# Weight tiles of 2048 columns in place of 1024 for the split into a rounded part and a remainder

## The chip, the cores and the metric

The kernel runs on one core of a Trainium2 chip, which stands alone on it. The metric is the device time of one execution in microseconds (us); the table below gives the median of three runs.

## What is computed

One layer of a hybrid decoder: 256 tokens of width 2048, in float32. A token mixer (an mLSTM group and an HGRN2 group that share one input projection and one output projection) and a SwiGLU network, each followed by a layer norm, each modulated by vectors that are worked out from a conditioning vector `c`. Cut to what matters here:

```python
mod = c_act @ w_mod[l] + b_mod[l]                       # 2048 x 12288
sh1, sc1, g1, sh2, sc2, g2 = jnp.split(mod[:, None, :], N_MOD, axis=-1)
u = x * (1.0 + sc1) + sh1
y = token_mixer(u, w_in[l], ..., w_out[l])              # u @ w_in, 2048 x 7176; y @ w_out, 2048 x 2048
x = layer_norm(DEEPNORM_ALPHA * x + (1.0 + g1) * y, ln1_g[l], ln1_b[l])
u = x * (1.0 + sc2) + sh2
y = swiglu(u, w_gate[l], w_up[l], w_down[l])            # 2048 x 5632 twice, 5632 x 2048
x = layer_norm(DEEPNORM_ALPHA * x + (1.0 + g2) * y, ln2_g[l], ln2_b[l])
```

## The kernel before

**Precision by splitting.** Weights and activations are float32. Each is written as a rounded part `h` and a remainder `l`, both in the type fp32r, and a product is the sum of three matmuls: rounded by rounded, rounded by remainder, remainder by rounded. So each weight passes through four steps: a DMA into a raw tile `wr` (on SyncE's queue, SP), a copy with rounding on ScalarE (ACT) into `wh`, the subtraction raw minus rounded on VectorE (DVE) into `wl`, and then the matmuls on TensorE (PE).

**Tiles.** Such a tile has 128 partitions and 1024 columns, 512 KB. There are 408 of them: 112 for the input projection, 32 for the output projection, 176 for gate and up, 88 for down. The pool of raw tiles has 4 buffers, those of `wh` and `wl` 5 each (line 56). A raw buffer comes free when the subtraction has read it; a `wh` or `wl` buffer when the last matmul on it is through. The helpers are `wtile` (line 203, input projection, two tiles for each 1 MB block of `in_win`) and `w1` (line 707, the other matrices); a copy shows in the profile as L128 with output `wh`, a subtraction as L213 (input projection) or L715 (the others), the loads as L208 and L710.

**Modulation.** 96 columns of `mod` are each made by loading a tile of 128x2048 of `w_mod` (1 MB, two buffers, `mr`) and one multiply-and-sum on VectorE over 2048 columns (L174). The first 32 feed `u` and have to be there before the input projection can use the rows they scale: `make_u` makes 128 rows of `u` (a scaled copy `t` and a rounding `uh` on ScalarE, a subtraction `ul` on VectorE). The other columns are spread over the later phases (`mods_some`, `some`).

**Phases.** The input projection starts with four rounds of 128 rows over the sections q and f (`fq_part`, eight PSUM banks; one round uses one 1 MB block, 48 matmuls of 256 columns), each round after the two modulation columns for its rows. Then come the sections qk, g, i and v for the same rows (`tile_part`: 1 MB blocks, again 48 matmuls of 256 columns, or 24 of 512 for i and v), then rows 512 to 1023, then the rest. PSUM is drained by ScalarE (or added up by VectorE) at the end of each block. The recurrences of HGRN2 and mLSTM run on VectorE, ScalarE and TensorE between the later blocks. Then the output projection (two passes over `c`, four column groups), the residual and the statistics of the first norm (`resid`, `stat`, `norm`), the transposes of the normed rows (`turn`, L817), gate and up for the first two groups together (`ffn_in((0, 1))`), the other nine groups (`up_to`), and down in two passes (`down`).

**Order.** Each engine works through its instructions in a fixed order, and so does SyncE, which issues all loads: an instruction that waits holds up all behind it. The order is set when the program is built, by a scheduler that takes the buffers of the pools and priorities into account; copies and subtractions of weights run under a raised priority (`PRI["w"]`).

Of the kernel before, what the change touches and what calls it, by code (L numbers as in the profile page):

```python
# [3 lines left out]
F32 = mybir.dt.float32  # L4
# [5 lines left out]
P = 128  # L10
# [42 lines left out]
PE_SECT = ()  # L53
DVE_SECT = ()
RATE = (0.45, 0.4, 0.5)
CFG = dict(big=10, med=10, wr=4, mr=2, wh=5, wl=5, s5=4, t=3, cm=2)


def win_plan():
# [20 lines left out]
def build(nc, tc, d):  # L80
    from contextlib import ExitStack

    with ExitStack() as ctx:
# [116 lines left out]
        def col(s, k):  # L200
            return modc[:, 16 * s + k : 16 * s + k + 1]

        def wtile(src, n=2048, cut=1024):
            for a in range(0, n, cut):
                m = min(cut, n - a)
                cnt[0] += 1
                r = wr.tile([P, 1024], F32, tag="w", name=f"wr{cnt[0]}")
                nc.sync.dma_start(r[:, :m], src[a // cut][:, :m])  # L208
                h = wh.tile([P, 1024], F32R, tag="h", name=f"wh{cnt[0]}")
                l = wl.tile([P, 1024], F32R, tag="l", name=f"wl{cnt[0]}")  # L210
                with tc.high_priority(PRI["w"]):
                    act(h[:, :m], r[:, :m], AF.Copy)
                    tt(l[:, :m], r[:, :m], h[:, :m].bitcast(F32), ALU.subtract)  # L213
                yield h, l

        def wraw(src):
            for a in range(2):
                cnt[0] += 1
                r = wr.tile([P, 1024], F32, tag="w", name=f"wr{cnt[0]}")
                nc.sync.dma_start(r, src[a])  # L220
                yield r, None

        def gN(bank, w, nk, n, u, k0, first, last):
            for b in range(n // P):
# [139 lines left out]
        def gates():  # L364
            raw = M(576, name="wg")
            nc.sync.dma_start(raw, d["wg"])
            h = wh.tile([P, 1024], F32R, tag="h", name="wgh")[:, :576]
            l = wl.tile([P, 1024], F32R, tag="l", name="wgl")[:, :576]
            with tc.high_priority(PRI["w"]):
                split(h, l, raw)  # L370
            o = psp.tile([P, 512], F32, tag="ps", name="gps")
# [332 lines left out]
                act(o[:, 512 * c : 512 * c + 512], bank, AF.Copy)  # L704
            return o

        def w1(src):
            cnt[0] += 1
            r = wr.tile([P, 1024], F32, tag="w", name=f"wr{cnt[0]}")
            nc.sync.dma_start(r, src)  # L710
            h = wh.tile([P, 1024], F32R, tag="h", name=f"wh{cnt[0]}")
            l = wl.tile([P, 1024], F32R, tag="l", name=f"wl{cnt[0]}")
            with tc.high_priority(PRI["w"]):
                act(h, r, AF.Copy)
                tt(l, r, h.bitcast(F32), ALU.subtract)  # L715
            return h, l

        def three(banks, h, l, a, b, first, last):
            for i, o in enumerate(banks):
                w = slice(512 * i, 512 * i + 512)  # L720
# [31 lines left out]
        def half(tiles, k, t):  # L752
            return tiles[k // 8][:, (k % 8) * T + t * P : (k % 8) * T + t * P + P]
# [4 lines left out]
        for part in (1, 0):  # L758
            for c in range(4):
                if part:  # L760
                    banks[c] = [ps(), ps()]
                tiles = []
                skew = part == 0 and c == 3
                for p in range(4):
                    tiles.append(w1(d["wo"][16 * (1 - part) + 4 * c + p]))
                    mods_some(RATE[2])
                    if not skew:
                        for t in range(2):
                            for j in range(2):
                                k = 8 * part + 2 * p + j  # L770
                                w = slice(512 * j, 512 * j + 512)
                                three([banks[c][t]], tiles[-1][0][:, w], tiles[-1][1][:, w], half(yh, k, t), half(yl, k, t), part == 1 and k == 8, part == 0 and k == 7)
                if skew:
                    for t in range(2):
                        for p in range(4):
                            for j in range(2):
                                k = 2 * p + j
                                w = slice(512 * j, 512 * j + 512)
                                three([banks[c][t]], tiles[p][0][:, w], tiles[p][1][:, w], half(yh, k, t), half(yl, k, t), False, k == 7)
                if part == 0:  # L780
                    for t in range(2):
                        resid(t, c, banks[c][t], G1, ALPHA)
                        stat(t, c)
# [105 lines left out]
        tc.add_manual_dep(table["load"], table["var"].name, order, reason="table")  # L889
        bk, held, block = ffn_in((0, 1))  # L890
        for k in range(2):
            for g in range(2):
                held[k, g] = w1(d["wf"][g * KT + k])
            block(k, 0)
        for c in range(4):
            turn(1, c)
# [2 lines left out]
        for k in range(2):  # L899
            block(k, 1)  # L900
        for k in range(2, KT):
            for g in range(2):
                held[k, g] = w1(d["wf"][g * KT + k])
            for t in range(2):
                block(k, t)
            some(2)
            for c in (2, 3):
                if k == 4 * c - 4:
                    some(max(0, len(late) - 8 * (3 - c)))
                    affine1(c)  # L910
                    make_u2(0, c)
                    make_u2(1, c)
# [15 lines left out]
        def up_to(gs):  # L928
            for g in gs:
                bk, held, block = ffn_in((g,))  # L930
                for k in range(KT):
                    held[k, g] = w1(d["wf"][g * KT + k])
                    for t in range(2):
                        block(k, t)
                    if k == 2:
# [10 lines left out]
        def down(k0, k1, G, last):  # L946
            for c in range(4):
# [7 lines left out]
                        three([bk[t]], held[k][0][:, w], held[k][1][:, w], hslice(k + j, t, 0), hslice(k + j, t, 1), k + j == k0, k + j == k1 - 1)  # L955

                for k in range(k0, k1, 2):
                    held[k] = w1(d["wd"][22 * c + k // 2])
                    if k < k1 - skew:
                        for t in range(2):  # L960
                            pair(k, t)
# [92 lines left out]
```

## Time and profile before

| what | us |
|---|---|
| median of 3 runs | 1266.17 (1265.77 to 1267.21) |
| the profiled execution, its own time | 1265.78 |
| its span, first to last instruction | 1264.0 |
| TensorE busy | 1212.8 (96%) |
| VectorE busy | 901.2 (71%) |
| ScalarE busy | 591.7 (47%) |
| DMA queue of the loads, share of the 16 engines | 74.9% |

The span is 1.8 us shorter than the time of the same execution. Matmuls are pipelined: the time of one matmul in the profile is longer than the distance to the next, so work on TensorE is counted below as matmuls times distance. TensorE is busy nearly always; VectorE is above 90% between 215 and 420 us and from 504 to 530 us, and at about half after 640 us. The granted clock of TensorE is 0.99 on the mean.

### The profile page before, as it was taken

To read this page: it belongs to the slowest core of one execution; us is meant where nothing else is said; L and a number is where in the kernel's file an instruction comes from. 1 tells how busy PE (TensorE), PEld (TensorE's weight loads), DVE (VectorE), ACT (ScalarE), POOL (GpSimd) and SP (SyncE) were. 2 spreads that over 40 slices of the span, in tenths; PEclk is the share of its full clock that TensorE was granted. 3 is DMA by queue.
4 is the path that set the end of the run, shared out by engine and by line. 5 is a ranking of instruction groups with operands and counts; after the bars stand their busy time and mean duration, and the time that the engine had idled before them with its cause. 6 is when DMAs were issued, how large, how long until landed. Compare 5 with 4: busy or idle time off the path is not lost.

```text
span 1264.0 us, 17132 instructions
## 1 busy us (share of the span) xinstructions
PE 1212.8 (96%) x6706; PEld 1040.0 (82%) x6706; DVE 901.2 (71%) x979; ACT 591.7 (47%) x743; POOL 3.9 (0%) x13
## 2 busy tenths in 40 slices
PE   4899999999999999799999999999999999999995
PEld 4888899997889887688888888888888888888884
DVE  6778997999999979997877554455555445445655
ACT  4554454835664644644544444433344444434340
POOL 0000000000000000000000000000000000000000
PEclk9999999999999999899999999999999999999998
DMA  9998997857788989889998666666666666676661
GB/s 364 386 335 328 341 398 285 301 200 264 267 327 308 330 317 334 305 320 327 324 329 325 192 190 189 178 194 191 198 191 192 189 194 185 193 256 184 191 191 66
DMA packets 75968, 328.00 MB, mean 260 GB/s; under 512 B 8432, under 2 KB 8816, under 8 KB 62704
## 3 DMA queue, kind: packets, MB, share of 16 engines
q1 hardware_dynamic: 75888, 326.92, 74.9%
q8 instruction: 52, 0.85, 0.3%
q14 instruction: 28, 0.23, 0.0%
HBM read 324.79 MB, written 2.10 MB: 259 GB/s over the span
## 4 chain that ended last, share of the span: by engine, by line
PE 89%; DVE 5%; ACT 3%; issue 2%; DMA 1%; DVEq 0%; ACTq 0%
PE ps L722 21%; PE ps L725 21%; PE ps L721 21%; PE ps L251 5%; PE ps L249 5%; PE ps L250 5%; PE ps L260 2%; PE ps L261 2%; PE ps L262 2%; DVE m L174 2%; PE ps L447 1%; ACT wh L128 1%; DMA m<-in_wmod 1%; DVE wl L213 1%; PE ps L863 1%
## 5 line engine op out<-in xcount | busy, mean ns | idle before, releaser
L128 ACT ACTIVATE wh<-wr 128x1024 fp32r<-128x1024 f32 x408 | 431.1, 1059 | 550.8 <-PE ps L722 426.2
L715 DVE TENSOR_TENSOR wl<-wr,wh 128x1024 fp32r<-128x1024 f32 x296 | 360.6, 1224 | 283.7 <-ACT wh L128 280.4
L721 PE MATMUL ps<-wh,u2h 128*128 128x512 f32 x704 | 275.6, 392 | 0.3 <-ACT s L128 0.3
L722 PE MATMUL ps<-wh,u2l 128*128 128x512 f32 x704 | 273.7, 389 | 0.1
L174 DVE CUSTOM_DVE_ANT_0 m<-m,cb,init 128x2048 f32<-128x2048 f32 x96 | 225.1, 2346 | 22.3 <-DMA m<-in_wmod 22.0
L725 PE MATMUL ps<-wl,u2h 128*128 128x512 f32 x704 | 217.0, 389 | 0.0
L249 PE MATMUL ps<-uh,wh 128*128 128x256 f32 x640 | 184.4, 292 | 22.5 <-ACT wh L128 17.1
L250 PE MATMUL ps<-ul,wh 128*128 128x256 f32 x640 | 181.8, 286 | 0.0
L251 PE MATMUL ps<-uh,wl 128*128 128x256 f32 x640 | 180.3, 287 | 1.1 <-DVE wl L213 1.0
L721 PEld LDWEIGHTS ps<-wh,u2h 128*128 128x128 f32 x704 | 132.6, 188 | 28.9 <-ACT s L128 0.7
L722 PEld LDWEIGHTS ps<-wh,u2l 128*128 128x128 f32 x704 | 132.0, 188 | 28.0 <-DVE u2l L838 0.8
L725 PEld LDWEIGHTS ps<-wl,u2h 128*128 128x128 f32 x704 | 132.1, 188 | 27.6
L213 DVE TENSOR_TENSOR wl<-wr,wh 128x1024 fp32r<-128x1024 f32 x112 | 135.8, 1221 | 25.1 <-ACT wh L128 24.5
L249 PEld LDWEIGHTS ps<-uh,wh 128*128 128x128 f32 x640 | 123.6, 194 | 25.0 <-ACT wh L128 17.8
L721 PE MATMUL ps<-wh,hid 128*128 128x512 f32 x352 | 137.2, 390 | 0.0
L725 PE MATMUL ps<-wl,hid 128*128 128x512 f32 x352 | 137.0, 389 | 0.0
L722 PE MATMUL ps<-wh,hid 128*128 128x512 f32 x352 | 137.0, 389 | 0.0
L250 PEld LDWEIGHTS ps<-ul,wh 128*128 128x128 f32 x640 | 124.5, 195 | 1.3 <-issue 1.0
L251 PEld LDWEIGHTS ps<-uh,wl 128*128 128x128 f32 x640 | 123.2, 194 | 1.9 <-DVE wl L213 1.8
L725 PEld LDWEIGHTS ps<-wl,hid 128*128 128x128 f32 x352 | 66.1, 188 | 13.9
L721 PEld LDWEIGHTS ps<-wh,hid 128*128 128x128 f32 x352 | 66.1, 188 | 13.6
L722 PEld LDWEIGHTS ps<-wh,hid 128*128 128x128 f32 x352 | 66.1, 188 | 13.6
(179 smaller groups left out, 1017.8 us busy)
## 6 DMA issues: line engine op xcount, KB each, us to landing
m<-in_wmod SPq DMA_DIRECT2D x96, 1024.0 KB, 7.1
wr<-in_wf SPq DMA_DIRECT2D x176, 512.0 KB, 4.2
wr<-in_win SPq DMA_DIRECT2D x112, 512.0 KB, 6.0
wr<-in_wd SPq DMA_DIRECT2D x88, 512.0 KB, 3.6
wr<-in_wo SPq DMA_DIRECT2D x32, 512.0 KB, 5.4
xT<-in_x SPq DMA_DIRECT2D x4, 512.0 KB, 8.0
z<-in_xr SPq DMA_DIRECT2D x2, 1024.0 KB, 8.6
out<-z SPq DMA_DIRECT2D x8, 256.0 KB, 2.4
```

The lines of the kernel that those rows point to most:

```text
L128: i = nc.scalar.activation(out, in_, f, **kw).ins
L174: table["mod"] = nc.vector.tensor_tensor_reduce(t, t, cb, 1.0, init[:, j : j + 1], ALU.mult, ALU.add, modc[:, j : j + 1]).ins
L213: tt(l[:, :m], r[:, :m], h[:, :m].bitcast(F32), ALU.subtract)
L249: mm(o, h[:, wsl], kt(uh, k0 + k), start=st, stop=False, skip_group_check=True)
L250: mm(o, h[:, wsl], kt(ul, k0 + k), start=False, stop=False, skip_group_check=True)
L251: mm(o, l[:, wsl], kt(uh, k0 + k), start=False, stop=en, skip_group_check=True)
L260: mm(o, a, h[:, w], start=first and k == 0, stop=False, skip_group_check=True)
L261: mm(o, a, l[:, w], start=False, stop=False, skip_group_check=True)
L715: tt(l, r, h.bitcast(F32), ALU.subtract)
L721: mm(o, a, h[:, w], start=first, stop=False, skip_group_check=True)
L722: mm(o, b, h[:, w], start=False, stop=False, skip_group_check=True)
L725: mm(o, a, l[:, w], start=False, stop=last, skip_group_check=True)
```

## The change

The helpers `wtile`, `wraw` and `w1` go; one helper `wide` takes one or two blocks of 1024 columns, loads each with a DMA of its own into one raw tile of 2048 columns, and rounds and subtracts the whole tile with one copy and one subtraction. It hands out halves of the two results. All loads keep their size and number (408 of 512 KB); copies and subtractions of weights go from 408 to 204 each. The pools change from 4, 5 and 5 buffers of 1024 columns to 2 (raw), 3 (rounded) and 2 (remainder) buffers of 2048. The input projection takes the two halves of a block of `in_win` as one tile, the first two groups of gate and up take the tiles of both groups for one k, the others those of two successive k, and the output projection and down two neighbouring tiles.

```diff
-CFG = dict(big=10, med=10, wr=4, mr=2, wh=5, wl=5, s5=4, t=3, cm=2)
+CFG = dict(big=10, med=10, wr=2, mr=2, wh=3, wl=2, s5=4, t=3, cm=2)
...
-        def wtile(src, n=2048, cut=1024):
...
+        def wide(*srcs):
+            cnt[0] += 1
+            n = 1024 * len(srcs)
+            r = wr.tile([P, 2048], F32, tag="w", name=f"wr{cnt[0]}")
+            for i, src in enumerate(srcs):
+                nc.sync.dma_start(r[:, 1024 * i : 1024 * i + 1024], src)
+            h = wh.tile([P, 2048], F32R, tag="h", name=f"wh{cnt[0]}")
+            l = wl.tile([P, 2048], F32R, tag="l", name=f"wl{cnt[0]}")
+            with tc.high_priority(PRI["w"]):
+                act(h[:, :n], r[:, :n], AF.Copy)
+                tt(l[:, :n], r[:, :n], h[:, :n].bitcast(F32), ALU.subtract)
+            return [(h[:, 1024 * i : 1024 * i + 1024], l[:, 1024 * i : 1024 * i + 1024]) for i in range(len(srcs))]
+
+        def wtile(src):
+            yield from wide(src[0], src[1])
...
-                    tiles.append(w1(d["wo"][16 * (1 - part) + 4 * c + p]))
+                    if p % 2 == 0:
+                        tiles += wide(*[d["wo"][16 * (1 - part) + 4 * c + p + i] for i in range(2)])
...
-            for g in range(2):
-                held[k, g] = w1(d["wf"][g * KT + k])
+            held[k, 0], held[k, 1] = wide(*[d["wf"][g * KT + k] for g in range(2)])
...
-                    held[k, g] = w1(d["wf"][g * KT + k])
+                    if k % 2 == 0:
+                        held[k, g], held[k + 1, g] = wide(*[d["wf"][g * KT + k + i] for i in range(2)])
...
-                    held[k] = w1(d["wd"][22 * c + k // 2])
+                    if (k - k0) % 4 == 0:
+                        held[k], held[k + 2] = wide(*[d["wd"][22 * c + k // 2 + i] for i in range(2)])
```

The scheduler lays the instructions out anew, and three places are of use below. In the names, `wl` is a remainder, `m` a tile of `w_mod` whose sum goes to `modc`, `t`, `uh` and `ul` the three steps of `make_u`.

VectorE, first two rounds of q and f, before:

```order
L213 TENSOR_TENSOR wl_143<-wr_140,wh_142 128x1024
L213 TENSOR_TENSOR wl_173<-wr_170,wh_172 128x1024
L174 ISA m_200,modc<-m_200,cb,init 128x2048
L174 ISA modc 128x1
L174 ISA m_203,modc<-m_203,cb,init 128x2048
L174 ISA modc 128x1
L213 TENSOR_TENSOR wl_213<-wr_210,wh_212 128x1024
L231 TENSOR_TENSOR ul_111<-t_206,uh_109 128x256
L213 TENSOR_TENSOR wl_243<-wr_240,wh_242 128x1024
```

VectorE at the same place, now:

```order
L213 TENSOR_TENSOR wl_144<-wr_140,wh_143 128x2048
L174 ISA m_195,modc<-m_195,cb,init 128x2048
L174 ISA modc 128x1
L174 ISA m_198,modc<-m_198,cb,init 128x2048
L174 ISA modc 128x1
L227 TENSOR_TENSOR ul_111<-t_201,uh_109 128x256
L213 TENSOR_TENSOR wl_209<-wr_205,wh_208 128x2048
L174 ISA m_260,modc<-m_260,cb,init 128x2048
```

A round's first half was subtracted ahead of `ul`; now the whole tile is subtracted behind it, and the next round's sums stand behind the whole tile.

ScalarE, where the sections q and f are drained and qk begins (`q`, `f`, `qk` from a PSUM bank `ps` are the drains), before:

```order
L128 ACTIVATE f_114<-ps_127 128x512
L128 ACTIVATE qk_117<-ps_431 128x512
L128 ACTIVATE wh_505<-wr_503 128x1024
L128 ACTIVATE qk_117<-ps_432 128x512
L128 ACTIVATE wh_535<-wr_533 128x1024
L128 ACTIVATE t_563<-xT_564,modc 128x256
L128 ACTIVATE uh_109<-t_563 128x256
L128 ACTIVATE wh_575<-wr_573 128x1024
L128 ACTIVATE qk_117<-ps_501 128x512
L128 ACTIVATE qk_117<-ps_502 128x512
L128 ACTIVATE wh_608<-wr_606 128x1024
```

ScalarE at the same place, now:

```order
L128 ACTIVATE f_114<-ps_127 128x512
L128 ACTIVATE qk_117<-ps_411 128x512
L128 ACTIVATE wh_481<-wr_478 128x2048
L128 ACTIVATE t_533<-xT_534,modc 128x256
L128 ACTIVATE qk_117<-ps_412 128x512
L128 ACTIVATE uh_109<-t_533 128x256
L128 ACTIVATE wh_546<-wr_543 128x2048
L128 ACTIVATE qk_117<-ps_476 128x512
L128 ACTIVATE qk_117<-ps_477 128x512
L128 ACTIVATE wh_608<-wr_605 128x2048
```

`wh_481` is the second tile of qk and `wh_546` the first of g: each copy of a whole tile now stands behind the drain of a block that TensorE works on.

VectorE at the end of the output projection (`s` and the first `z` are a residual, `st` the statistics, `mv` their sum, and the last two `wl` of each fence are weights of gate and up), before:

```order
L715 TENSOR_TENSOR wl_5016<-wr_5013,wh_5015 128x1024
L715 TENSOR_TENSOR wl_5034<-wr_5031,wh_5033 128x1024
L732 TENSOR_TENSOR s_4922<-ps_4512,bc_4246 128x512
L715 TENSOR_TENSOR wl_5040<-wr_5037,wh_5039 128x1024
L715 TENSOR_TENSOR wl_5118<-wr_5115,wh_5117 128x1024
L736 SCALAR_TENSOR_TENSOR z_4240<-z_4240,s_4922 128x512
L732 TENSOR_TENSOR s_4926<-ps_4513,bc_4246 128x512
L739 BN_STATS st_4244<-z_4240 128x6
L736 SCALAR_TENSOR_TENSOR z_4241<-z_4241,s_4926 128x512
L743 BN_AGGR mv_4944<-st_4244 128x2
L174 ISA m_5235,modc<-m_5235,cb,init 128x2048
```

VectorE at the same place, now:

```order
L174 ISA m_4853,modc<-m_4853,cb,init 128x2048
L174 ISA modc 128x1
L213 TENSOR_TENSOR wl_4651<-wr_4647,wh_4650 128x2048
L717 TENSOR_TENSOR s_4562<-ps_4202,bc_3966 128x512
L717 TENSOR_TENSOR s_4566<-ps_4203,bc_3966 128x512
L721 SCALAR_TENSOR_TENSOR z_3960<-z_3960,s_4562 128x512
L721 SCALAR_TENSOR_TENSOR z_3961<-z_3961,s_4566 128x512
L724 BN_STATS st_3964<-z_3960 128x6
L724 BN_STATS st_3965<-z_3961 128x6
L213 TENSOR_TENSOR wl_4670<-wr_4666,wh_4669 128x2048
L728 BN_AGGR mv_4584<-st_3964 128x2
L728 BN_AGGR mv_4630<-st_3965 128x2
```

Both halves of the tokens are now summed up together, and a second whole tile of weights stands between the statistics and their sum.

## Rows read from the trace of the kernel before

**Rows 1.** The page: engine, busy us (share of span) xinstructions

```profile
PE 1212.8 (96%) x6706; PEld 1040.0 (82%) x6706; DVE 901.2 (71%) x979; ACT 591.7 (47%) x743; POOL 3.9 (0%) x13
```

**Rows 2.** Waits of TensorE: who waited for whom, us, times, longest

```profile
PE ps L249 <- ACT wh L128: 17.1, 3, 16.7
PE ps L249 <- ACT uh L128: 5.3, 2, 3.8
PE ps L817 <- DVE z L810: 8.2, 1, 8.2
```

**Rows 3.** Busy time by stage: window, length, engines' busy us (xcount), clock, DMA share, GB/s

```profile
51.00:145.00 94.00, 91.26 (x577) 81.87 (x576) 79.94 (x81) 48.78 (x65) 0.74 (x1) 1.00 0.90 336
145.00:215.00 70.00, 70.00 (x586) 69.92 (x585) 58.78 (x58) 33.65 (x38) 0.74 (x1) 1.00 0.90 347
215.00:420.00 205.00, 200.85 (x1678) 180.23 (x1677) 194.61 (x256) 120.50 (x202) 0.00 (x0) 0.99 0.78 280
504.00:530.00 26.00, 17.42 (x77) 13.47 (x77) 25.97 (x40) 14.88 (x33) 0.00 (x0) 0.80 0.83 305
640.00:1245.00 605.00, 605.00 (x2714) 501.72 (x2713) 322.76 (x301) 250.97 (x257) 0.00 (x0) 1.00 0.65 201
```

**Rows 4.** Groups by line: engine, op, shapes, xcount, busy us, mean ns, idle before

```profile
L715 DVE TENSOR_TENSOR wl<-wr,wh 128x1024 fp32r<-128x1024 f32 x296 | 360.6, 1224 | 283.7 <-ACT wh L128 280.4 <-PE ps L863 3.0
L174 DVE CUSTOM_DVE_ANT_0 m<-m,cb,init 128x2048 f32<-128x2048 f32 x96 | 225.1, 2346 | 22.3 <-DMA m<-in_wmod 22.0
...
L128 ACT ACTIVATE wh<-wr 128x1024 fp32r<-128x1024 f32 x408 | 431.1, 1059 | 550.8 <-PE ps L722 426.2 <-DMA wr<-in_win 48.7 <-PE ps L250 38.4
```

**Rows 5.** Timeline, first 52 us, VectorE and ScalarE: start, length, instruction, idle before

```profile
15.57 1.99 ACT L128 ACTIVATE wh<-wr 128x1024 fp32r<-128x1024 f32 x2
...
18.92 2.34 DVE L174 CUSTOM_DVE_ANT_0 m<-m,cb,init 128x2048 f32<-128x2048 f32 x1
...
26.77 2.35 DVE L174 CUSTOM_DVE_ANT_0 m<-m,cb,init 128x2048 f32<-128x2048 f32 x1
29.27 2.35 DVE L174 CUSTOM_DVE_ANT_0 m<-m,cb,init 128x2048 f32<-128x2048 f32 x1
...
31.66 0.60 ACT L128 ACTIVATE t<-xT,modc 128x256 f32<-128x256 f32 x1 [0.18 <-DVE modc L174]
32.29 0.42 ACT L128 ACTIVATE uh<-t 128x256 fp32r<-128x256 f32 x1
...
35.80 2.35 DVE L174 CUSTOM_DVE_ANT_0 m<-m,cb,init 128x2048 f32<-128x2048 f32 x1 [0.88 <-DMA m<-in_wmod]
...
51.24 0.59 ACT L128 ACTIVATE f<-ps 128x512 f32<-128x512 f32 x1
```

**Rows 6.** Loads issued from 44 to 160 us: GB/s in 40 slices, us to landing

```profile
GB/s 429 407 424 384 205 424 362 136 429 370 353 348 268 340 326 381 374 387 158 394 401 384 407 316 376 360 143 410 233 403 364 384 266 251 370 291 347 398 333 400
...
wr<-in_win SPq DMA_DIRECT2D x40, 512.0 KB, 5.8
m<-in_wmod SPq DMA_DIRECT2D x17, 1024.0 KB, 7.0
```

**Rows 7.** Loads issued from 640 to 1240 us: xcount, KB each, us to landing

```profile
wr<-in_wd SPq DMA_DIRECT2D x88, 512.0 KB, 3.6
```

**Rows 8.** Timeline from 504 to 513 us: end of the output projection, first norm

```profile
504.05 2.35 DVE L715 TENSOR_TENSOR wl<-wr,wh 128x1024 fp32r<-128x1024 f32 x2
506.32 0.68 DVE L736 SCALAR_TENSOR_TENSOR z<-z,s 128x512 f32<-128x512 f32 x1
...
508.71 0.25 DVE L743 BATCH_NORM_AGGREGATE mv<-st 128x2 f32<-128x24 f32 x1
508.89 2.28 DVE L174 CUSTOM_DVE_ANT_0 m<-m,cb,init 128x2048 f32<-128x2048 f32 x1
...
511.70 1.89 DVE L810 TENSOR_SCALAR z<-z,mv 128x512 f32<-128x512 f32 x4
512.28 3.67 PE L817 MATMUL ps<-kc,z 128*128 128x128 f32 x16 [8.17 <-DVE z L810]
```

More of the change, by code (lines that the diff above doesn't have):

```diff
@@ L201, in col @@
             return modc[:, 16 * s + k : 16 * s + k + 1]
-        def wtile(src, n=2048, cut=1024):
[L204 to L221, printed above, removed]
+        def wide(*srcs):
[12 more added lines that the diff above has]
+            yield from wide(src[0], src[1])
         def gN(bank, w, nk, n, u, k0, first, last):
@@ L366, in gates @@
             nc.sync.dma_start(raw, d["wg"])
-            h = wh.tile([P, 1024], F32R, tag="h", name="wgh")[:, :576]
-            l = wl.tile([P, 1024], F32R, tag="l", name="wgl")[:, :576]
+            h = wh.tile([P, 2048], F32R, tag="h", name="wgh")[:, :576]
+            l = wl.tile([P, 2048], F32R, tag="l", name="wgl")[:, :576]
             with tc.high_priority(PRI["w"]):
@@ L705, in bcast @@
             return o
[L707 to L716, printed above, removed]
         def three(banks, h, l, a, b, first, last):
@@ L771, in build @@
                                 w = slice(512 * j, 512 * j + 512)
-                                three([banks[c][t]], tiles[-1][0][:, w], tiles[-1][1][:, w], half(yh, k, t), half(yl, k, t), part == 1 and k == 8, part == 0 and k == 7)
+                                three([banks[c][t]], tiles[p][0][:, w], tiles[p][1][:, w], half(yh, k, t), half(yl, k, t), part == 1 and k == 8, part == 0 and k == 7)
                 if skew:
@@ L901, in build @@
         for k in range(2, KT):
-            for g in range(2):
-                held[k, g] = w1(d["wf"][g * KT + k])
+            held[k, 0], held[k, 1] = wide(*[d["wf"][g * KT + k] for g in range(2)])
             for t in range(2):
@@ L931, in up_to @@
                 for k in range(KT):
-                    held[k, g] = w1(d["wf"][g * KT + k])
+                    if k % 2 == 0:
+                        held[k, g], held[k + 1, g] = wide(*[d["wf"][g * KT + k + i] for i in range(2)])
                     for t in range(2):
```

## The prediction

> **What bounds the kernel now.** I read the page's shares first, then what TensorE waits for, then the busy time by stage. TensorE is busy for 96% of the span [rows 1]. Its idle time is in few places [rows 2]: 16.7 us before the first matmul, some 5 us in the first rounds while u is made, and 8.2 us at the first norm; the rest is mostly the tail after the last matmul, where VectorE finishes the second norm. From 640 to 1245 us TensorE never idles, and VectorE works 323 of 605 us [rows 3]. Two stages are tight on both: from 51 to 145 us the loads take 0.90 of the DMA engines while TensorE idles only 2.7 us, and from 215 to 420 us VectorE is busy 194.6 of 205 us while TensorE idles 4.2 [rows 3]. So the reader should see that almost nothing is to be won on ScalarE or VectorE, and that TensorE stays fed because weights lie ready ahead: the copy into wh waits 426 us in all for TensorE to give a buffer back [rows 4], that is, the five buffers stand full.
>
> **What the change saves.** 204 copies and 204 subtractions fewer, at the same bytes and matmuls. A subtraction of 1024 columns takes 1.224 us, a VectorE operation on 2048 columns 2.346 [rows 4]; so a whole tile saves 2 x 1.224 - 2.35 = 0.1 us, 20 us of VectorE in the run. Two copies in a row take 1.99 us [rows 5]; I take 1.95 for a copy of 2048 and 2.3 for a subtraction. These savings lie beside TensorE's work wherever weights are ready ahead, so I cost them at nothing; where that cover is gone, they are inside the sums below.
>
> **What it costs.** A tile is usable only when its second load has landed and the whole copy is done, and remainders have 2 buffers: the next tile's subtraction cannot start before TensorE has left the tile before the present one. The lead falls from four tiles of 1024 (some 11 us) to one of 2048, minus its own subtraction (some 3 us).
>
> *First rounds (rows of u 0 to 511).* In the new order each round is a closed ring on VectorE and ScalarE: two sums, t, uh, ul, the whole copy (behind uh), the whole subtraction, and behind that the next sums. Sums: 4.6 us (2 x 2.28); t and uh 1.05; copy 1.95; subtraction 2.3; handovers 0.2: 10.1 us. Before, the sums of successive rounds begin at 18.92, 26.77 and 35.80, so 7.9 and 9.0 us apart, since half a tile was copied ahead of t and uh [rows 5]. The new first tile: copy from about 15.8 to 17.75, subtraction to 20.1; sums at 20.1, 30.2, 40.3; fourth copy from 40.3 + 4.6 + 0.1 + 1.05 = 46.05 to 48.0. TensorE runs 10 matmuls on the rounded part (1.2 us at 0.12 each, from 586 in 70 us [rows 3]), waits for the remainder until 50.35, then 38 more, 4.55 us: 54.9. Before, the last drain of this round starts at 51.24 [rows 5], right behind matmuls that end at about 50.5. **+4.4 us**; bounds 3 (a copy starts earlier than I have it) and 6 (sums' loads, 7.0 us to land [rows 6], come late).
>
> *51 to 145 us, the sections for the first rows.* Now two raw buffers make a ring: subtraction done, load issued, second half landed, copy, subtraction. A load of 512 KB lands after 5.8 us; at the best rate of the stage, 429 GB/s, the second half adds 1.2 [rows 6]. 0.1 + 5.8 + 1.2 + 1.95 + 0.1 + 2.3 = 11.45 us for two tiles, 5.7 each. TensorE needs 48 x 0.12 = 5.76 for a tile of q, f, qk or g, and 24 x 0.223 = 5.35 for one of i or v (0.223: 605 us over 2714 matmuls [rows 3]). The margin is nothing, and each drain (0.59 us [rows 5]) ahead of a copy or sum (2.35) ahead of a subtraction comes on top. I chained the sixteen tiles by hand in the new order with these durations: TensorE waits 1.4 us at the second tile of qk, 2.6 at the first tile of the second set of rows (its last u waits for two sums), and 0.2 to 1.6 at four more; 7.5 in all, where it loses 2.7 in idle time now and somewhat more in slow starts. **+4 us**, bounds 1 and 12 (half a microsecond a tile more).
>
> *145 to 215 us.* The same ring with one or two sums a round; TensorE does not idle here now [rows 3]. **+2**, bounds 0 and 5.
>
> *215 to 420 us.* In the new order VectorE has 62 us of work from the 38th subtraction to the 46th, while TensorE has 58 between the same tiles; over twenty tiles both are near 157. Without a lead of four tiles, bursts of the recurrences hit TensorE. The stage has no row for that; bounds are 0 and the 10.4 us in which VectorE idles today for its own dependencies [rows 3], if TensorE had to stand for as long. The stage's sums are nearly even, so I take the lower half: **+4**.
>
> *Output projection into the first norm.* In its last four column groups VectorE gets 2.3 + 2.35 + three steps of a residual (started 0.6 apart, as the row of z and the next in [rows 8]) = 6.45 us a tile against 5.4 on TensorE. With one tile of lead that puts the end of the projection back by 1.5. Then, today, TensorE stops at 504.1, the statistics are summed at 508.71, one more sum (2.28) comes first, and transposes start at 512.28, 8.17 us after the stop [rows 8]. In the new order the end of two sums of modulation (0.5), a subtraction (2.3), six residual steps (3.6), another subtraction (2.3), the sums of the statistics of both halves (0.5), one more sum of modulation (2.4) and the normalization (0.6) stand there: counted from the stop, the transposes start at 12.2. The second half of the tokens then follows 1.5 us closer, and one tile of gate and up comes 0.6 late. 1.5 + 4.0 - 1.5 + 0.6 = **+4.6**, bounds 0 (the sums find their place beside the matmuls) and 8.
>
> *640 us on.* Ring: 0.1 + 3.6 + 1.2 + 1.95 + 0.1 + 2.3 = 9.25 for two tiles [rows 7] against 2 x 24 x 0.223 = 10.7: **0**, covered by TensorE's own work; bounds 0 and +3 at the turns of groups. The tail after the last matmul is the same: **0**.
>
> Sum: 4.4 + 4 + 2 + 4 + 4.6 = 19 us on the profiled execution's 1265.8 (span 1264.0 and 1.8 around it), 0.4 under the median: **1285 us**.
>
> **A rule against and a rule for.** VectorE and ScalarE have idle time (71% and 47% busy [rows 1]), yet what TensorE waits for is their work. For such engines, not saturated but the cause of bubbles elsewhere, the Trainium skill, Perfetto Trace Analysis, section Optimizing Scalar/DVE Operations, advises to break instructions up; this change merges them, and by that rule the sum would be over zero, as mine.
>
> **Rivals.** *Faster: the saved fixed cost decides.* 0.1 us less for each tile on VectorE matters where it is full: 26 tiles from 215 to 420 us give 2.6, ten around the norm 1, and some of the 4.2 us of idle there could go; the first rounds could give 1 to 2. 1265.8 - 6 = 1260 us. Against it: TensorE idles little in those stages, and not for weights [rows 2, 3]. The Trainium skill, VectorE: DVE Perf Modes, section on the TRN2 errata, states that a single large tile pays the fixed latency once where many small ones pay it each; the two rows above agree on the sign. *No change: the first rounds' lag vanishes* because loads set the pace there and the later buffers, though fewer, suffice: 1266. Against it: the ring of the first rounds is longer than any load. *Slow everywhere: the two raw buffers bind in the long stage too.* If the second half lands 2 us later than in the sum above, the ring is 11.25 against 10.7, 0.27 us for each of 112 tiles from 640 us on, 30 us, and the earlier stages reach their upper bounds: 1265.8 + 30 + 25 = 1321. Against it: the loads use 0.65 of the DMA engines there.
>
> **How the numbers follow.** My forecast 0.80; faster 0.07; no change 0.08; slow everywhere 0.05. The measurement can tell about 0.2%, 2.5 us. The lower bounds of my terms give 4 us, the upper 34, but not all at one end: 1270 to 1302 holds the time 8 times in 10. Faster 0.07, within 0.2% 0.08, slower 0.85.
>
> **What would show it.** Right: sums of the first rounds about 10 us apart, drains of f ending near 55 us; waits of TensorE for copies or remainders of weights in many places from 51 to 215 us; VectorE's subtraction waiting for TensorE in place of ScalarE's copy; transposes of the first norm some 5 us later relative to their stage than the lag before; no idle TensorE after 640 us. Wrong: sums 8 to 9 us apart, TensorE without new waits before 215 us, or idle time in every tile of the down projection.

## The result, and the profile after

The changed kernel takes 1276.49 us (median of 4 runs, 1274.71 to 1277.16), the kernel before 1266.13 in the same comparison: a ratio of 1.0079 (95% interval 1.0067 to 1.0091), 10.4 us slower. The prediction was 1285 (1270 to 1302), slower with 0.85: the sign and the range held, the size was 8.5 us too high. The profiled execution of after has a span of 1275.3 us, 11.3 more than before.

The page of after, shares of the span and two groups by line (as [rows 1, 4]):

```profile
PE 1215.7 (95%) x6706; PEld 1042.5 (82%) x6706; DVE 879.5 (69%) x775; ACT 553.8 (43%) x539; POOL 3.9 (0%) x13
...
L213 DVE TENSOR_TENSOR wl<-wr,wh 128x2048 fp32r<-128x2048 f32 x204 | 467.2, 2291 | 305.5 <-PE ps L710 214.5
L128 ACT ACTIVATE wh<-wr 128x2048 fp32r<-128x2048 f32 x204 | 390.7, 1916 | 553.9 <-DMA wr<-in_wf 265.0
```

The change does what it says. VectorE works 21.7 us less and ScalarE 37.9 less than in [rows 1]; the subtraction now waits for TensorE (214.5 us) where the copy waited for it before [rows 4]. Neither engine's saving reaches the end. What TensorE waits for (as [rows 2]; us in total, times, longest), after:

```profile
PE ps L245 <- ACT wh L128: 25.0, 5, 17.4
PE ps L803 <- DVE z L796: 10.8, 1, 10.8
PE ps L247 <- DVE wl L213: 3.4, 3, 1.6
PE ps L706 <- DVE s L839: 2.7, 1, 2.7
PE ps L257 <- DVE wl L213: 2.3, 2, 1.2
```

The waits for copies rise from 17.1 to 25.0 us, but the 5.3 us for `uh` [rows 2] are gone: in the first rounds TensorE now waits for a copy that stands behind `uh`, so the two together grow by 2.6 us. Those for remainders (L247, L257) are 5.7 us against 2.3, and L706 is a wait that before did not have. The wait at the first norm (L803) is 10.8 against 8.17 us. By stage (as [rows 3], windows moved along with the lag):

```profile
55.00:149.00 94.00, 87.66 (x554) 79.18 (x554) 73.10 (x62) 45.54 (x47) 0.75 (x1) 0.98 0.83 317
149.00:220.00 71.00, 70.71 (x571) 69.71 (x570) 54.86 (x43) 27.98 (x23) 0.74 (x1) 1.00 0.92 351
220.00:425.00 205.00, 203.94 (x1719) 184.04 (x1718) 197.11 (x237) 123.04 (x183) 0.00 (x0) 1.00 0.78 283
650.00:1256.00 606.00, 606.00 (x2719) 502.61 (x2718) 309.32 (x192) 231.46 (x150) 0.00 (x0) 1.00 0.57 199
```

TensorE idles 6.3 of 94 us in the second stage (2.7 before), and its granted clock there is 0.98 of 2.4 GHz (1.00 before). It idles 1.1 us in the recurrences (4.2 before, so better), and never from 650 us on.

Where the time went is seen best by laying the traces side by side: both hold the same 5856 matmuls on weights, so the start of the n-th in one minus that in the other is the lag there. Its growth by stage, in us (stages by the time of the kernel before; e1 to e12 are the experiments; all from one profiled execution each, whose own time lies between 3.6 us under and 1.8 us over the median of its kernel, so small differences between sums say nothing):

| kernel | 0-50 | 50-143 | 143-302 | 302-321 | 321-484 | 484-591 | 591-638 | 638 on | sum |
|---|---|---|---|---|---|---|---|---|---|
| after | 4.1 | 4.9 | 0.1 | -5.0 | 0.8 | 1.9 | 4.6 | 0 | 11.4 |
| e1 halves | 0.7 | 2.5 | -0.1 | 1.6 | 0.7 | 0.4 | -0.1 | 0 | 5.7 |
| e2 whole in the input projection | 3.2 | 4.8 | 0.1 | -4.9 | 0.2 | -0.3 | -0.1 | 0 | 3.0 |
| e3 whole behind it | 0.6 | 2.4 | 0 | 0.5 | 1.0 | 2.1 | 0 | 0 | 6.6 |
| e4 1024, pools 4/6/4 | -1.4 | 0 | 5.9 | -5.0 | 0.9 | -1.0 | 0 | 0 | -0.6 |
| e5 product first | 4.5 | 3.4 | 0.2 | -5.0 | 0.6 | 1.4 | 1.5 | 0 | 6.6 |
| e6 third raw buffer | 3.9 | 4.8 | 0.5 | -1.2 | 0.6 | -2.4 | 0 | 0 | 6.2 |
| e7 third remainder buffer | 3.8 | 4.8 | 0.6 | -4.9 | 1.4 | 0.5 | 0 | 0 | 6.2 |
| e8 1024, products first | 2.4 | 0 | 0 | -3.7 | 1.0 | 0.8 | -0.1 | 0 | 0.4 |
| e9 order of the first rounds | 3.8 | 3.4 | 0.4 | -5.0 | 1.7 | 2.0 | 1.4 | 0 | 7.7 |
| e10 the same, on e2 | 6.2 | 3.5 | 0.2 | -4.9 | 0.6 | -1.1 | 0 | 0 | 4.5 |
| e11 halves, third raw buffer | -1.4 | 2.4 | 0.4 | 0.5 | 0.3 | -2.3 | 0 | 0 | -0.1 |
| e12 1024, asked for in pairs | 0.3 | 2.4 | 6.5 | -3.7 | 2.0 | 0.5 | 0 | 0 | 8.0 |

So after loses mainly in four places, gains in one, and the second half of the program is unchanged to 0.1 us.

### The profile page after: what moved, and what is told of

It is laid out like the page before. It is cut to its first block, busy times and chain, and to the rows that moved or that the text cites. A ratio compares the mean times of both kernels' runs of the same rounds, so it can differ in the third digit from the quotient of the medians.

```text
span 1275.3 us, 16453 instructions
## 1 busy us (share of the span) xinstructions
PE 1215.7 (95%) x6706; PEld 1042.5 (82%) x6706; DVE 879.5 (69%) x775; ACT 553.8 (43%) x539; POOL 3.9 (0%) x13
## 4 chain that ended last, share of the span: by engine, by line
PE 88%; DVE 7%; issue 2%; ACT 2%; DMA 1%; DVEq 0%; SPq 0%; ACTq 0%
PE ps L706 20%; PE ps L710 20%; PE ps L707 20%; PE ps L247 6%; PE ps L246 6%; PE ps L245 5%; DVE wl L213 3%; PE ps L257 2%; PE ps L256 2%; PE ps L258 2%; DVE m L174 2%; ACT wh L128 1%; PE ps L443 1%; DMA wr<-in_wo 1%; PE ps L849 1%
## 5 line engine op out<-in xcount | busy, mean ns | idle before, releaser
L213 DVE TENSOR_TENSOR wl<-wr,wh 128x2048 fp32r<-128x2048 f32 x204 | 467.2, 2291 | 305.5 <-PE ps L710 214.5
L128 ACT ACTIVATE wh<-wr 128x2048 fp32r<-128x2048 f32 x204 | 390.7, 1916 | 553.9 <-DMA wr<-in_wf 265.0
L706 PE MATMUL ps<-wh,u2h 128*128 128x512 f32 x704 | 275.9, 393 | 2.7 <-DVE s L839 2.7
L247 PE MATMUL ps<-uh,wl 128*128 128x256 f32 x640 | 177.8, 288 | 3.6 <-DVE wl L213 3.4
L706 PEld LDWEIGHTS ps<-wh,u2h 128*128 128x128 f32 x704 | 132.9, 189 | 30.8 <-DVE s L839 3.1
L706 PE MATMUL ps<-wh,hid 128*128 128x512 f32 x352 | 137.2, 390 | 0.0
L247 PEld LDWEIGHTS ps<-uh,wl 128*128 128x128 f32 x640 | 122.3, 196 | 5.1 <-DVE wl L213 4.5
L706 PEld LDWEIGHTS ps<-wh,hid 128*128 128x128 f32 x352 | 66.1, 188 | 13.6
L257 PE MATMUL ps<-wl,uh 128*128 128x512 f32 x128 | 50.2, 392 | 2.3 <-DVE wl L213 2.3
```

The source lines that it names most:

```text
L128: i = nc.scalar.activation(out, in_, f, **kw).ins
L213: tt(l[:, :n], r[:, :n], h[:, :n].bitcast(F32), ALU.subtract)
L247: mm(o, l[:, wsl], kt(uh, k0 + k), start=False, stop=en, skip_group_check=True)
L257: mm(o, a, l[:, w], start=False, stop=False, skip_group_check=True)
L706: mm(o, a, h[:, w], start=first, stop=False, skip_group_check=True)
```

## Experiments

Each ratio is to the kernel before, timed in the same comparison.

**e1, halves.** The pools of the change, but two copies and two subtractions for each tile:

```diff
-                act(h[:, :n], r[:, :n], AF.Copy)
-                tt(l[:, :n], r[:, :n], h[:, :n].bitcast(F32), ALU.subtract)
+                step = 1024
+                for a in range(0, n, step):
+                    s = slice(a, a + step)
+                    act(h[:, s], r[:, s], AF.Copy)
+                    tt(l[:, s], r[:, s], h[:, s].bitcast(F32), ALU.subtract)
```

> The changed kernel with its pools (2 raw, 3 rounded, 2 remainder buffers of 2048 columns), but each tile copied and subtracted in two halves of 1024 columns. Theory A (the length of the operations): it takes a whole copy of 1.9 us and a whole subtraction of 2.3 us to bring a tile to TensorE where two halves overlap, and what stands behind them on VectorE waits longer; with halves the lag of 4.1 us in the first rounds, the 4.9 us from 54 to 149 us, the 1.9 us at the first norm and the 4.6 us at the turn of the first groups go, and the time is 1261 (if the 4.9 us that the changed kernel gained near 310 us stay) to 1267. Theory B (the buffers): raw, rounded and remainder buffers come free only in pairs, so fewer loads run ahead; halves change nothing and the time is 1274 to 1278.

Measured 1.0024 (1.001 to 1.0037), 1269.65 us. TensorE's waits, e1:

```profile
PE ps L248 <- ACT wh L128: 16.6, 2, 16.3
PE ps L806 <- DVE z L799: 6.4, 1, 6.4
PE ps L248 <- ACT uh L128: 6.1, 2, 3.8
PE ps L493 <- DVE q L477: 3.6, 1, 3.6
```

Some 7 of the 10.4 us go, although the buffers are those of the change, so the pools alone do not make the loss (B falls). The wait at L706 is gone. In the first rounds TensorE waits 6.1 us for `uh`, where in after it waits 6.6 for copies. But the edit also lays out a new order, and the table shows that not all of the gain is the length of the operations (A): the 4.6 us at 614 us hang on order, as e3 and e5 show, and so do the 5.0 us near 310 us that are lost again here. Against A stand, too, the 2.5 us that stay from 50 to 143 us.

**e2 and e3, one part alone.** The loop of e1, with `nw` the count of tiles so far; e2, and e3 the other way round:

```diff
-                step = 1024
+                step = n if nw[0] <= 56 else 1024
```

> Whole tiles of 2048 columns in the input projection, as in the changed kernel; copies and subtractions in halves from the output projection on, same pools. Theory A: the first 150 us keep their 9 us, the gain of 4.9 us near 310 us stays, the losses at the norm (1.9) and at the turn of the first groups (4.6) go: 1266 + 9 - 4.9 = 1270, and 1269 to 1272 with what cannot be told. Theory B: 1274 to 1278, as the changed kernel.

> The other part alone: copies and subtractions in halves in the input projection, whole ones from the output projection on, same pools. Theory A: 1.9 us at the norm and 4.6 at the turn of the first groups on top of what the kernel with halves everywhere takes: that kernel plus 5 to 7 us. Theory C: those two losses were an accident of the order that the scheduler laid out, not of the tile's size; then it is within 2 us of the kernel with halves everywhere.

Measured 1.0021 (1.0012 to 1.0029) and 1.0045 (1.0033 to 1.0058). e2 came out as A had it: 3.2 + 4.8 - 4.9 and nothing behind. e3 is 2.7 us over e1 by the ratios, and the table shows why it is not the expected 5 to 7: whole operations take 2.1 us at the norm (0.4 with halves), but nothing at the turn of the first groups. There theory C is right: after's 4.6 us hang on its order.

**e4, 1024 columns with the bytes of the new pools.** `CFG`: wr=4, wh=6, wl=4.

> The kernel before with tiles of 1024 columns and pools of the bytes of the changed kernel: 4 raw, 6 rounded, 4 remainder buffers (5 and 5 before). Theory A: with short operations one remainder buffer less costs nothing: 1264 to 1268, and up to 5 us less if the stall of 3.1 us at 308.8 us goes with the order that is laid out anew. Theory B (the lead in remainders counts): 1270 or more, with waits of TensorE for remainders from 51 to 145 us.

Measured 1.0017 (1.0007 to 1.0028). One remainder buffer less loses nothing from 50 to 143 us (B falls), and near 310 us 5.0 us are gained with small tiles. What it loses instead is new: until 261.9 us TensorE waits 3.7 us for a product of the recurrence (L456) that the new order put behind a sum of modulation and a subtraction. Its profiled execution was the fastest of twelve, 3.6 us under the median, so the table shows it that much too well.

**e5, the product ahead.** In after, `swi`:

```diff
-            act(s, gate, AF.Silu)
-            tt(s, s, up, ALU.mult)
+            with tc.high_priority(PRI["w"] + 100):
+                act(s, gate, AF.Silu)
+                tt(s, s, up, ALU.mult)
```

> The changed kernel with one thing more: the SiLU copy and the product of gate and up (which free the PSUM banks) get a priority above the copies and subtractions of weights, so that at the turn from the first two groups to the third the first product stands ahead of the subtraction that it waited behind. Theory A: the loss of 4.6 us at 614 to 624 us (2.7 us of wait and the half clock behind it) hangs on one order of two instructions; it goes, and the time is 1276.5 - 4.6 = 1272 (ratio to the kernel before 1.0045). Theory B: VectorE is behind at this place as a whole, and TensorE then waits as long for the remainder that was moved back: 1275 to 1277.

Measured 1.0057 (1.0044 to 1.0069). The place in after, VectorE and TensorE:

```profile
612.14 2.35 DVE L174 CUSTOM_DVE_ANT_0 m<-m,cb,init 128x2048 f32<-128x2048 f32 x1 [4.09 <-DMA m<-in_wmod]
...
614.42 2.29 DVE L213 TENSOR_TENSOR wl<-wr,wh 128x2048 fp32r<-128x2048 f32 x1
...
616.63 0.68 DVE L839 TENSOR_TENSOR s<-s,ps 128x512 f32<-128x512 f32 x1
...
617.36 0.78 PE L706 MATMUL ps<-wh,u2h 128*128 128x512 f32 x1 [2.70 <-DVE s L839]
...
617.93 0.63 PE L707 MATMUL ps<-wh,u2l 128*128 128x512 f32 x1
```

The first two groups hold all eight PSUM banks; the third cannot start before a product has emptied one, and the product stood behind a sum (2.35) and a whole subtraction (2.29). Behind the wait of 2.70 us a matmul takes 0.63 in place of 0.39: the granted clock is 0.72 of 2.4 GHz from 616 to 622 us, thus the level of 1.2 GHz for a part of it. Busy time and clock of that stretch:

```profile
616.00:622.00 6.00, 4.64 (x13) 3.74 (x14) 5.68 (x7) 2.72 (x5) 0.00 (x0) 0.72 0.75 269
```

With the product ahead 1.5 of the 4.6 us stay, 1.3 of them a wait for the remainder that now comes later. Both theories are partly right. That e3, e6 and e7, with whole tiles here too, lose nothing in this place shows that tile size does not force it.

**e6 and e7, a third buffer.** After with med=8 and wr=3 (e6), or med=8 and wl=3 (e7).

> The changed kernel with a third raw buffer (8 instead of 10 small buffers of the med pool make room). Theory A1 (the ring of two raw buffers, load after subtraction, makes the 4.9 us from 54 to 149 us): a third buffer takes that away, the lag at 145 us falls from 9.0 to 4 or 5 us, and the time is 1272. Theory A2 (the order on ScalarE and VectorE makes it: a whole copy behind the scaled copies of u, a whole subtraction in one round with two sums): the lag at 145 us stays at 8 to 9 us, 1275 to 1277. The first rounds keep 4 us by both.

> The changed kernel with a third remainder buffer in place of a third raw one (8 med buffers again). Theory A1: as the subtraction no longer waits for TensorE, raw buffers come free earlier; 2 to 5 us less in the first 150 us, and the losses at the norm (1.9) and at the turn of the first groups (4.6) go, 1266 to 1271. Theory A2: the first 150 us keep 8 to 9 us; at the norm and the turn only the order decides, 1270 to 1277.

Measured 1.0058 (1.0045 to 1.0071) and 1.0041 (1.0028 to 1.0055). A1 falls in both: from 50 to 143 us both lose 4.8 as after does (4.9). They are faster than after only further on, where the order is laid out anew. TensorE's waits for remainders in e6 are those of after, to 0.2 us:

```profile
PE ps L247 <- DVE wl L213: 3.2, 3, 1.6
PE ps L257 <- DVE wl L213: 2.3, 2, 1.2
```

**e8, the stall of before taken away by order.** In the kernel before:

```diff
-                tt(k4[:, :, 0, :], k4[:, :, 0, :], d3[:, :, 1:2].broadcast_to([P, n, c]), ALU.mult)
-                tt(g4[:, :, 1, :], g4[:, :, 1, :], d3[:, :, 0:1].broadcast_to([P, n, c]), ALU.mult)
+                with tc.high_priority(PRI["w"] if c == 64 else 0): tt(k4[:, :, 0, :], k4[:, :, 0, :], d3[:, :, 1:2].broadcast_to([P, n, c]), ALU.mult)
+                with tc.high_priority(PRI["w"] if c == 64 else 0): tt(g4[:, :, 1, :], g4[:, :, 1, :], d3[:, :, 0:1].broadcast_to([P, n, c]), ALU.mult)
```

> The kernel before, tiles of 1024 columns, with one thing changed: in the recurrence of HGRN2 the two products of the last level get the priority of the weights, so that the second one no longer stands behind two subtractions where TensorE waits 3.1 us for it at 308.8 us. Theory A (the 4.9 us that the changed kernel gained there were an accident of order, not of the tile): most of it is gained here too, 1266 - 2.5 (wait) - up to 2.4 (half clock) = 1261 to 1264. Theory B (only fewer operations on VectorE can give it): the wait moves to the next place, 1265 to 1267.

Measured 0.9985 (0.9976 to 0.9994), 1265.0 us: the fastest of all, faster than both kernels. The time alone lies at the edge of B's range. The place is A's: the wait falls from 3.1 to 1.0 us, and 3.7 us are gained there. In the profiled execution 2.4 us are lost in the first rounds, with the instructions of before. What it takes away stands in the trace of the kernel before, VectorE and TensorE:

```profile
306.16 2.35 DVE L174 CUSTOM_DVE_ANT_0 m<-m,cb,init 128x2048 f32<-128x2048 f32 x1
...
308.43 1.22 DVE L213 TENSOR_TENSOR wl<-wr,wh 128x1024 fp32r<-128x1024 f32 x1
309.57 0.68 DVE L477 TENSOR_TENSOR kk<-kk,f 128x512 f32<-128x512 f32 x1
310.30 1.23 DVE L213 TENSOR_TENSOR wl<-wr,wh 128x1024 fp32r<-128x1024 f32 x1
311.44 0.68 DVE L478 TENSOR_TENSOR q<-q,f 128x512 f32<-128x512 f32 x1
...
312.27 1.46 PE L494 MATMUL ps<-q,kk 128*128 128x128 f32 x8 [3.10 <-DVE q L478]
```

The product q stood behind two subtractions. In after, only one sum of modulation stands ahead of the pair, and q comes with no subtraction in between. With tiles of 1024 columns e8, e4 and e12 gain 3.7 to 5.0 us here; with tiles of 2048 e1, e3, e6 and e11 have a wait of 3.5 or 3.6 us here again. The gain is one of order, not of the tile.

**e9 and e10, the order of the first rounds written out.** In after (e9) and e2 (e10), `fq_part` asks for the weights between the two sums of a round; `make_u` moreover ties its scaled copy behind the copy of the weights:

```diff
...
+                if 0 < k < 4:
+                    run(mod(16 + todo.pop(0)))
+                    first = table["mod"]
+                    win = list(next_win())
+                    tc.add_manual_dep(ahead["rem"], first.name, order, reason="weights")
+                    prep(k + 1)
+                    tc.add_manual_dep(table["mod"], ahead["rem"].name, order, reason="weights")
...
```

> The changed kernel, whole tiles everywhere, with the order of the first four rounds written out: the load and the copy of the next whole tile stand ahead of the scaled copy of u, and its subtraction between the two sums of a round. Theory A (the 4.1 us of the first rounds come from a ring in which a whole copy and a whole subtraction stand one behind the other after u): a round is then second sum 2.35, t and uh 1.05, copy beside the next first sum 2.35, subtraction 2.3, thus 8 us in place of 9.76, until the loads bind; the lag after the first rounds falls from 4.1 to between -1 and 1, and the time from 1276.5 to 1272 to 1274. Theory B (the longer wait for the second half of the load makes it): the lag stays at 3 to 4 us, 1275 to 1277.

> The kernel with whole tiles in the input projection alone and halves behind it, with the same order of the first four rounds. It was at 1.0021 of the kernel before without that order. Theory A: 3 to 4 us less, 1263 to 1266, at or under the kernel before. Theory B: 1268 to 1269, as without it.

Measured 1.0049 (1.0035 to 1.0063) and 1.0016 (1.0007 to 1.0025): the first rounds keep 3.8 and 6.2 us, not the -1 to 1 of A. The ring of operations was opened, and another wait took its place. SyncE's queue and ScalarE, e9:

```profile
14.53 7.81 SPq L173 DMA_DIRECT2D m<-in_wmod  x2
22.52 0.80 SPq L210 DMA_DIRECT2D wr<-in_win  x2
...
29.54 1.91 ACT L128 ACTIVATE wh<-wr 128x2048 fp32r<-128x2048 f32 x1 [1.65 <-DMA wr<-in_win]
```

The second of two loads of `w_mod` waits on SyncE's queue until its buffer is free at 22 us, and the loads of the next weights wait behind it, though their buffer is free from 19.7 us on, when its subtraction ended; the copy then waits for them, at 29.5 and again later. In that order the loads set the pace. That B (the second half alone) is right does not follow: the two orders differ in more than that.

**e11, halves with a third raw buffer.** e1 with med=8, wr=3.

> Halves everywhere with a third raw buffer (8 small buffers in place of 10). With halves and two raw buffers the copies wait for loads from 75 to 102 us, and 2.5 us are lost there. Theory A1 (with short operations the raw buffers that come free in pairs bind): those 2.5 us go, the lag at 145 us falls from 3.2 to about 1 us, and the time from 1269 to 1266 to 1267. Theory A2 (the loads' rate binds, whatever the buffers): 1268 to 1270.

Measured 1.001 (1.0001 to 1.0019). The time is near A1's, and yet A1 falls: 2.4 us are lost from 50 to 143 us as with two raw buffers; what it gains stands in the first rounds and at the norm.

**e12, tiles of 1024, asked for in pairs.** The kernel before with `return list(wtile(d["win"][i]))` in place of the generator.

> The kernel before, tiles of 1024 columns and its own pools (4, 5, 5), with one thing of the change: in the input projection the two tiles of a block are asked for together, so that both loads are placed in one go on the queue of loads and the loads of modulation columns stand behind both. Halves with the pools of the change lost 2.4 to 2.5 us from 54 to 149 us, with two raw buffers and with three. Theory P (buffers that come free in pairs make that loss): nothing is lost here in that stretch, the lag grows by under 1 us from the end of the first rounds to 145 us. Theory G (asking for two at once, and with it the order of the loads, makes it): the lag grows by 2 to 3 us there. What the recurrences do with the new order near 310 us is open; the time is between 1262 and 1270.

Measured 1.0047 (1.0035 to 1.006). From 50 to 143 us it loses the 2.4 us of e1 and e11, with small tiles and the pools of before: asking for two at once makes that loss (G). Through the order of the loads, as G has it, it does not come, as the trace shows. ScalarE, before:

```profile
74.64 1.06 ACT L128 ACTIVATE wh<-wr 128x1024 fp32r<-128x1024 f32 x1
78.25 0.60 ACT L128 ACTIVATE i<-ps 128x512 f32<-128x512 f32 x1 [2.56 <-PE ps L262]
```

and ScalarE and TensorE, e12:

```profile
78.01 0.60 ACT L128 ACTIVATE i<-ps 128x512 f32<-128x512 f32 x1 [3.07 <-PE ps L262]
78.50 1.05 ACT L128 ACTIVATE wh<-wr 128x1024 fp32r<-128x1024 f32 x1
...
79.61 0.73 PE L260 MATMUL ps<-wh,uh 128*128 128x512 f32 x2 [0.28 <-ACT wh L128]
80.87 0.50 PE L261 MATMUL ps<-wl,uh 128*128 128x512 f32 x1 [0.52 <-DVE wl L213]
```

Asking for both tiles of a block at once also puts their copies and subtractions in another place. Before, one more tile was copied ahead of the drain of i. In e12 a copy stands behind that drain, for which ScalarE waits 3.07 us for TensorE, and TensorE then waits for the copy and for its remainder. The same follows one block later, from 84.83 us on. The copies begin right behind the drains, so no load holds them up there. The order of the loads changes too (two loads of modulation columns stand together at 82.65 us), but no wait shows that it costs anything. Most of the rest of e12's loss has nothing to do with the tile: 6.5 us between 143 and 302 us, where L456 is late as in e4.

## Why the prediction was right, and where not

**First rounds, +4.4: measured 4.1.** The ring is there as worked out. VectorE and ScalarE of after (as [rows 5]):

```profile
19.63 2.35 DVE L174 CUSTOM_DVE_ANT_0 m<-m,cb,init 128x2048 f32<-128x2048 f32 x1
...
24.92 0.42 ACT L128 ACTIVATE uh<-t 128x256 fp32r<-128x256 f32 x1
25.25 1.90 ACT L128 ACTIVATE wh<-wr 128x2048 fp32r<-128x2048 f32 x1
...
27.18 2.29 DVE L213 TENSOR_TENSOR wl<-wr,wh 128x2048 fp32r<-128x2048 f32 x1 [1.38 <-ACT wh L128]
...
29.39 2.34 DVE L174 CUSTOM_DVE_ANT_0 m<-m,cb,init 128x2048 f32<-128x2048 f32 x1
...
39.14 2.35 DVE L174 CUSTOM_DVE_ANT_0 m<-m,cb,init 128x2048 f32<-128x2048 f32 x1
...
52.51 2.74 ACT L128 ACTIVATE f<-ps 128x512 f32<-128x512 f32 x4
```

Sums at 19.63, 29.39 and 39.14 against 20.1, 30.2 and 40.3 forecast; the last drain ends at 55.25, forecast 55. The ring was in fact shorter than forecast and TensorE slower: the remainder of the fourth tile is there at 49.03 us, forecast 50.35, and the 38 matmuls behind it take 5.4 us in place of 4.55, at a granted clock of 0.72 of 2.4 GHz from 46 to 52 us. In five profiles with whole tiles there and the scheduler's own order the term is 3.2 to 4.5; with small operations it is -1.4 to 2.4 in six. That spread is not one of order: e8 has the instructions of before in this stretch and is 2.4 us later, with a longer wait for u (4.8 against 3.8 us) and a granted clock of 0.72 against 0.86 from 40 to 52 us, so a difference of some 2 us in one profile of this stretch says nothing.

**51 to 145 us, +4: measured 4.9.** The largest waits came where I had chained them by hand. ScalarE and TensorE of after:

```profile
57.54 0.60 ACT L128 ACTIVATE qk<-ps 128x512 f32<-128x512 f32 x1 [2.28 <-PE ps L247]
58.03 1.90 ACT L128 ACTIVATE wh<-wr 128x2048 fp32r<-128x2048 f32 x1
...
62.31 0.39 PE L247 MATMUL ps<-uh,wl 128*128 128x256 f32 x1 [1.46 <-DVE wl L213]
...
102.11 0.39 PE L245 MATMUL ps<-uh,wh 128*128 128x256 f32 x1 [0.95 <-ACT wh L128]
...
104.44 0.39 PE L247 MATMUL ps<-uh,wl 128*128 128x256 f32 x1 [1.58 <-DVE wl L213]
```

At the second tile of qk the whole copy stands behind a drain that waits for TensorE, and TensorE waits 1.46 us (forecast 1.4). At the first tile of the second set of rows the whole copy stands behind `t` and `uh`, which wait for two sums, and TensorE waits 0.95 and 1.58 us (forecast 2.6). In all it idles 6.3 us in the stage, against 7.5. What was wrong is the ring: I let two raw buffers bind, and a third moves none of these waits (1.46, 0.95 and 1.59 us in e6). The 2.4 us of e1, e11 and e12 are another loss and no part of the 4.9: they arise from 79 to 88 us, where after has no wait.

The match of 4 and 4.9 is in part luck, since some 1.4 us of it are TensorE's clock, for which no term of the sum stands. e5 has the instructions of after in the same order up to 320 us and the same waits at this place, and loses 3.4. Busy time and clock, after and then e5:

```profile
100.00:112.00 12.00, 9.46 (x60) 8.72 (x59) 8.23 (x7) 6.75 (x6) 0.61 (x1) 0.86 0.69 267
100.00:112.00 12.00, 9.47 (x71) 8.67 (x70) 8.81 (x8) 7.08 (x7) 0.75 (x1) 1.00 0.70 262
```

The granted clock is 0.86 of 2.4 GHz here in after, e2, e6 and e7, which lose 4.8 or 4.9 us in the stage, and 1.00 in e5, e9 and e10, which lose 3.4 or 3.5. Why it falls in some executions and not in others stays open.

**145 to 215 us, +2: 0.5.** Too careful; TensorE waits 0.3 us once, at 218 us.

**215 to 420 us, +4: measured -5.3 (9.5 us of lag at 215, 4.2 at 425).** This is the step that failed. I looked for bursts of the recurrences that a shorter lead would let through to TensorE, and did not ask what became of the one stall that the stage already had: 3.1 us from 309 us on (shown under e8), and behind it matmuls at 0.63 in place of 0.39 us until 316, at a granted clock of 0.86 from 309 to 321 us. It hung on two subtractions in front of one product, and any new order could remove or keep it. This one removed it. No rule in the sum could give the sign; the built order could, since it shows what stands ahead of that product.

**Output projection into the first norm, +4.6: measured 2.6 from 425 us on.** The list of what stands ahead of the transposes was right. VectorE and TensorE of after (as [rows 8]):

```profile
509.21 2.28 DVE L213 TENSOR_TENSOR wl<-wr,wh 128x2048 fp32r<-128x2048 f32 x1
...
515.01 2.27 DVE L213 TENSOR_TENSOR wl<-wr,wh 128x2048 fp32r<-128x2048 f32 x1
...
517.58 2.34 DVE L174 CUSTOM_DVE_ANT_0 m<-m,cb,init 128x2048 f32<-128x2048 f32 x1
...
520.45 3.67 PE L803 MATMUL ps<-kc,z 128*128 128x128 f32 x16 [10.81 <-DVE z L796]
```

Two subtractions and one sum, each 2.3 us, stand there, and the wait is 10.8 us against 12.2 forecast. 1.9 of the 2.6 come from 484 us on. Order counts as much as size there: the same stretch takes -2.4 to 2.1 us with whole tiles in the output projection, -2.3 to 0.8 without.

**640 us on, 0: 0,** but the turn before it, at 614 us, cost 4.6 us that stand nowhere in the sum: 2.7 us of wait and the slower matmuls behind it. I bounded such turns at 3 us, and only behind 640.

Put together: 4.1 + 4.9 + 0.5 - 5.3 + 2.6 + 4.6 = 11.4 against a sum of 19. The two terms of the first 145 us came out at 9.0 against 8.4; the rest was forecast at 10.6 and came out at 2.4, so the error lies in the stages where the order decides. That the time still fell into the range owes something to luck: a gain of 5.3 and a loss of 4.6 us, neither of them in the sum, nearly cancel.

Two additions of the prediction are off. The upper bounds of its terms give 44 us, not 34 (6 + 12 + 5 + 10.4 + 8 + 3), and the stages ahead of 640 us at their upper bounds give 41 us in the last rival, not 25, so 1337 in place of 1321. The upper end of the range was closer than the terms allowed.

**The rule against** held. For engines that are not saturated but hold up another, the Trainium skill, Perfetto Trace Analysis, section Optimizing Scalar/DVE Operations, says that breaking up instructions may allow work to be completed sooner. The runs agree: with the same buffers, halves run at 1.0024 and whole tiles at 1.0079. Rows of this case show why the rival of the saved fixed cost failed: VectorE works 21.7 us less in all, 0.1 us for a tile as the rival had it, and that is little against waits of 1 to 3 us for one longer operation.

## What to carry to other kernels

Here, merging operations that feed a busy engine saved time on engines that do not bound, and was paid where the work ahead of the bound engine has no lead: at the start, and wherever its inputs are made one round ahead. A change of tile size also changes the order in which loads are asked for and in which a scheduler lays out the rest; one product in front of or behind a subtraction or a sum was worth 3.7 to 6 us here, against 10.4 for the whole change. So split the edit (buffers, size of operations, order of requests), compare the traces by the lag of the same matmuls, and look whether the largest stall of the kernel before is there at all in the new order.

## What the runs showed that I had not expected

A wait of TensorE can cost more than its length, and the same wait not always the same. Behind the 3.1 us at 309 us (before) and the 2.7 us at 614.7 us (after) matmuls take 0.63 in place of 0.39 us for 3 to 4 us, and the lag of the place is 1.9 us more than the wait. But near 310 us a wait of 3.58 us is followed by a granted clock of 0.72 in e1 and 0.86 in e3 (12 us from 312 us on), and one of 3.51 us in e6 by 1.00 (12 us from 318 us on); the lag there grows by 1.6 and 0.5 us and falls by 1.2. So one profile can be off by some 3 us at such a place.

And the load queue passes a wait on: in e9 a load that waits until 22 us for its buffer keeps the weight loads behind it, whose buffer is free 2.8 us before they start, from starting, so that opening one ring closed another.
